# A new end for a hybrid decoder step: both normalisation factors as a power on GpSimd, low products last, all f32 products together, late scaling from two PSUM banks

## The chip, the core and the metric

The kernel runs on one core of one Trainium2 chip, as one program. The metric is the device time of one execution in microseconds (us). Three runs of the kernel before gave 1370.75, 1370.55 and 1371.1 us, so the median is 1370.75 us.

The engines are named as in the profile: PE (matrix products; PEld is its weight load), DVE (vector), ACT (scalar and activation functions), POOL (GpSimd), and SP, whose queue issues all of the transfers between main memory and the on-chip memory here. PSUM is the small memory in banks into which PE accumulates; an `acc` tile in this kernel is one bank of 128 partitions by 512 f32 numbers.

## The reference

One layer of a decoder step for 256 prompt tokens and 8 sample tokens, with 2048 features and everything in f32. The change concerns only the last lines, the residual of the channel mixer and the final normalisation:

```python
def rms_norm(x, g):
    xf = x.astype(jnp.float32)
    y = xf * lax.rsqrt(jnp.mean(xf * xf, axis=-1, keepdims=True) + EPS)
    return (y * g.astype(jnp.float32)).astype(x.dtype)
...
    x = x + (g_a * y_pool + g_b * y_lru + g_c * y_conf) @ w_out
    hid = jnp.square(jax.nn.relu(rms_norm(x, g_mlp) @ w_up))
    x = x + hid @ w_down
...
    y_prompt = rms_norm(xp, g_final)
    y_sample = rms_norm(xs, g_final)
```

So every token needs one number, its factor: the mean of its 2048 squares plus a small constant, to the power of minus one half. It can only be computed when the last of the 2048 features of that token is there.

## The kernel before, in words

**Layout.** All N = 264 tokens are worked on together. Activations lie feature by feature: the residual stream is `X`, 128 partitions by KD = 16 feature tiles by 264 tokens. Weights come in as a stream of chunks of 128 by 1024 numbers; ACT casts each into a high part `whi` and DVE subtracts to get the low part `wlo` (lines 223 and 224). An f32 product is made of three products of the rounded parts: high weight by high activation, low weight by high activation, high weight by low activation (`mm3`, line 250). An activation tile lies as a pair, 264 low numbers and then 264 high ones, and `rhs(k)` is this pair for k tile k. Four work queues are filled by hand in program order; on each engine instructions run in that order, and a semaphore wait holds up everything behind it on its engine.

**The last group.** The last four feature tiles of `w_down` (numbers 12, 13, 15, 14, in this order) are computed one after the other by `last_group`, so that each can be finished early; chunk c is half of a tile's 16 k tiles. For the last two (c = 4 to 7) the tokens are split. EARLY are the 136 tokens 128 to 263, LATE the 128 tokens 0 to 127. `early_mm` makes two products per k tile: the high weight with the EARLY columns of both activation parts (line 907; the two sums lie in columns 0 to 135 and 264 to 399 of the bank), and the low weight with all 264 high activations (line 908; columns 136 to 399). What is missing then for the LATE tokens are the two products with the high weight.

**The end** (`end`, called after chunk 7) finishes both kinds of tokens:
- EARLY tokens stay feature by feature. DVE adds the two sums of tile 14 to `X` (`plus`, line 911), squares them (line 1008); PE sums squares over partitions by a product with a matrix of 1/D (`early_sum`, line 951: once for `sq2`, which holds the squares of the other 15 tiles, once for tile 14). ACT takes the root of the mean (line 965, from a table of reciprocal roots loaded 1.28 us long at line 1189), DVE improves it by one Newton step (`early_factor`, lines 969 to 971), then multiplies `X` by it in five pieces, each followed by its store (`early_out`, lines 981 and 983).
- LATE tokens of the last two tiles are computed token by token: `late_rows` (line 961) uses the activations as weights and streams the high weights of both tiles, 32 products of 256 columns into the bank `turned`, whose first 256 columns are `pair`. `residual` (line 954) adds what is already in `X` by a product with the identity. Tiles 0 to 13 are turned by 14 transposes (`turn`, line 988) into four more banks. The squares of the first 14 tiles come from `sq2` by a product with one column (line 1002) and are copied by ACT (line 1003, `rest`); those of the pair by ACT with an accumulator (line 1021, `own`). ACT takes the root (line 965), DVE improves it in three steps on one column (`late_factor`, lines 975 to 977). ACT and DVE then scale the banks (lines 995, 993, 1030), and five stores follow (line 998).

The Newton step leaves out a factor of -1/2, which `gfin` (line 1146) and `last_gain` have in them instead.

Of the kernel before, what the change touches and what calls it, by code (L numbers as in the profile page):

```python
# [21 lines left out]
KD = D // P  # L22
EPS = 1e-6
LN_EXP = "natural_log_exp_and_others"
ROOT = "abs_reciprocal_sqrt_and_small"
GELU_C = 1.5957691216057308
GELU_K = 0.044715

# [65 lines left out]
def hybrid_step(ctx: ExitStack, tc: tile.TileContext, first, par_in, st_in, wall, y_out, st_out):  # L94
# [26 lines left out]
    gfin = cpool.tile([P, KD], F32, name="gfin")  # L121

    def pv(name, i=None, n=1):
        a, b = PCOL[name]
# [766 lines left out]
        later(1 + m % 4 // 2, one)  # L891
        later(2 + m % 4 // 2, other)

    ident = G[:, 12, :P]
    EARLY, NE = slice(P, N), N - P
    LATE = slice(0, P)
    wide = {}
# [3 lines left out]
    def apart(x):  # L901
        return x.rearrange("p (h n) -> p h n", h=2)

    def early_mm(ps, hi, lo, x, first, last):
        o = ps[:, :N + NE]
        both_sums = bass.AP(o.tensor, o.offset, [o.ap[0], [N, 2], [1, NE]])
        nc.tensor.matmul(both_sums, hi, apart(x)[:, :, EARLY], start=first, stop=False, skip_group_check=True)  # L907
        nc.tensor.matmul(ps[:, NE:NE + N], lo, x[:, N:], start=False, stop=last, skip_group_check=True)  # L908

    def plus(m, s, ps):  # L910
        nc.vector.tensor_tensor(X[:, m, s], X[:, m, s], ps, op=ALU.add)

    def gain(m, s):
        nc.scalar.activation(X[:, m, s], X[:, m, s], AF.Copy, scale=gfin[:, m:m + 1])

    def last_group(i, c, rhs, fn):
        t, k0 = c // 2, c % 2 * 8
        m = KD - 4 + LAST[t]
        if k0 == 0:
            wide[t] = acc()  # L920
        ps = wide[t]
        for k in range(k0, k0 + 8):
            s = slice((k - k0) * P, (k - k0 + 1) * P)
            hi, lo = whi[:, i % NHI, s], wlo[:, i % NHI, s]
            if c < 4:
                mm3(ps, hi, lo, rhs(k), k == 0, k == 15, MIXED)
            else:
                early_mm(ps, hi, lo, rhs(k), k == 0, k == 15)
        if c % 2 and t < 2:
            fn(t, ps)  # L930
        elif c == 5:
            plus(m, slice(0, N), ps[:, NE:NE + N])
            plus(m, EARLY, ps[:, :NE])
            nc.scalar.activation(squares[m][:, EARLY], X[:, m, EARLY], AF.Square)
            nc.gpsimd.tensor_tensor(sq2[:, EARLY], sq2[:, EARLY], squares[m][:, EARLY], op=ALU.add)
            gain(m, EARLY)
        elif c == 7:
            end(i, rhs)

    def end(i, rhs):  # L940
        assert i % NHI == 1 and NHI == 4
        m, fac, tn = KD - 2, G[:, 10, :], G[:, 9, :]
        unit = {}
        out = [cpool.tile([P, 4 * PITCH], F32, name=f"y{h}", tag=f"B{h}") for h in range(2)]
        turned, early, late = acc(), acc(), acc()
        pair = turned[:, :2 * P]
        halves = whi.rearrange("p (a b) c -> p a b c", a=2)
        own, rest, both_sq = late[:, 1:2], tn[:, 1:2], tn[:, 2:3]

        def early_sum(t, k):  # L950
            nc.tensor.matmul(early[:, :NE], ones, t[:, EARLY], start=k == 0, stop=k == 1)  # L951

        def residual(m, first, last):
            nc.tensor.matmul(turned[:, (m - KD + 2) * P:(m - KD + 3) * P], X[:, m, LATE], ident, start=first,  # L954
                             stop=last, skip_group_check=True)

        def late_rows(a, b):
            for k in range(a, b):
                w = halves[:, :, k // 8, k % 8 * P:k % 8 * P + P]
                for at in (0, N):  # L960
                    nc.tensor.matmul(apart(pair), rhs(k)[:, at:at + P], w, start=False, stop=False,  # L961
                                     skip_group_check=True)

        def root(dst, x, bias=0.0, scale=1.0):
            nc.scalar.activation(dst, x, AF.Abs_reciprocal_sqrt, bias=bias, scale=scale)

        def early_factor():
            s, r, t = early[:, :NE], rstd[:, EARLY], tn[:, EARLY]
            nc.vector.tensor_tensor(t, s, r, op=ALU.mult)
            nc.vector.tensor_tensor(t, t, r, op=ALU.mult)  # L970
            nc.vector.scalar_tensor_tensor(fac[:, EARLY], t, -3.0, r, op0=ALU.add, op1=ALU.mult)

        def late_factor():
            r = rstd[:, 0:1]
            nc.vector.scalar_tensor_tensor(both_sq, own, 1.0 / D, rest, op0=ALU.mult, op1=ALU.add)
            nc.vector.scalar_tensor_tensor(both_sq, both_sq, r, r, op0=ALU.mult, op1=ALU.mult)
            nc.vector.scalar_tensor_tensor(fac[:, 0:1], both_sq, -3.0, r, op0=ALU.add, op1=ALU.mult)

        def early_out(a, n):
            to = out[1][:, a * NE:(a + n) * NE]  # L980
            nc.vector.tensor_tensor(to.rearrange("p (k n) -> p k n", k=n), X[:, a:a + n, EARLY],
                                    fac[:, None, EARLY].to_broadcast([P, n, NE]), op=ALU.mult)
            nc.sync.dma_start(y_out[:, D + a * NE:D + (a + n) * NE], to)

        def turn(a, n):
            u = unit[a] = acc()
            for k in range(n):
                nc.tensor.transpose(u[:, k * P:(k + 1) * P], X[:, a + k, LATE], ident)  # L988

        def scale(eng, u, a, n):  # L990
            to, x, by = out[0][:, a * P:(a + n) * P], unit[u][:, (a - u) * P:(a - u + n) * P], fac[:, 0:1]
            if eng is nc.vector:
                nc.vector.tensor_scalar(to, x, by, None, op0=ALU.mult)  # L993
            else:
                nc.scalar.activation(to, x, AF.Copy, scale=by)  # L995

        def store(a, n):
            nc.sync.dma_start(y_out[:, a * P:(a + n) * P], out[0][:, a * P:(a + n) * P])

        ps = wide[3]  # L1000
        early_sum(sq2, 0)
        nc.tensor.matmul(late[:, :1], sq2[:, LATE], ones[:, :1], start=True, stop=True)  # L1002
# [5 lines left out]
        nc.vector.tensor_tensor(squares[m][:, EARLY], x, x, op=ALU.mult)  # L1008
# [12 lines left out]
        nc.scalar.activation(G[:, 14, :2 * P], pair, AF.Square, accum_out=own)  # L1021
# [8 lines left out]
        nc.vector.scalar_tensor_tensor(out[0][:, 14 * P:D], pair, fac[:, 0:1], last_gain, op0=ALU.mult, op1=ALU.mult)  # L1030
# [13 lines left out]
    def down_evac(q, m, whole):  # L1044
        into_x(m, whole)
        spend(dve=0.4)
        if q == 3:
            def rest():
                square_add(m)
                if m == 0:  # L1050
                    nc.gpsimd.tensor_scalar(sq2, sq2, 1.0, EPS * D / P, op0=ALU.mult, op1=ALU.add)  # L1051
                nc.scalar.activation(X[:, m, :], X[:, m, :], AF.Copy, scale=gfin[:, m:m + 1])

            later(0 if m >= KD - 4 else 1 + m % 4 // 2, rest)

# [79 lines left out]
    for i, ch in enumerate(chunks):  # L1135
# [6 lines left out]
        if i == 12:  # L1142
            softplus()
            again = first[:, KD:KD + 4 * HEAD].rearrange("p (k c) -> p k c", k=4)[:, :, :N]
            nc.sync.dma_start(X[:, 0:4, :], again)
            nc.vector.tensor_scalar(gfin, pv("g_final"), -0.5, None, op0=ALU.mult)
        if i % 2 == 0:
            dma_pair((i + 8) // 2)
        if i == 2:
# [32 lines left out]
            grp_mm(i)  # L1182
        if i == len(chunks) - 64:
            make_identity(nc, ident)
            nc.sync.dma_start(last_gain, par_in[:, NPAR:])
        if i == len(chunks) - 32:
            nc.scalar.activation(last_gain, last_gain, AF.Copy, scale=-0.5)
# [120 lines left out]
```

## Time and profile before

| what | us |
|---|---|
| median of three runs | 1370.75 |
| lowest and highest run | 1370.55, 1371.1 |
| span of the profiled execution, first to last instruction | 1368.7 |
| last product of the `early_mm` stream done | 1356.31 |
| last product on PE done (transposes) | 1362.75 |
| last instruction on DVE done | 1364.56 |
| transfers to main memory run dry | about 1367.2 |

The profile holds one execution, whose own time is given as its span, 1368.7 us; that is 2.05 us less than the median of the runs, which also count what lies before the first and after the last instruction. All times named with a decimal position such as "1356.31" are microseconds from the start of this span. A row of the timeline reads: start, duration, engine, line and operation, and in brackets how long the engine had been idle before and what ended it; consecutive instructions of one line are merged into one row. The chain of waits is a list of the work that ended last, with start and duration of each piece. A row of the table by stretches has the stretch, and for each engine its busy time and, in brackets, how many instructions; then the granted clock, the busy share of the transfer engines and what they moved in GB/s.

### The profile page before, as it was taken

The page shows a single profiled execution, that of the slowest core. Times are in us where ns is not written, and L with a number is a line of the kernel's source. Part 1 is how long each engine was busy: PE and PEld are TensorE (multiplying, and loading weights), DVE is VectorE, ACT ScalarE, POOL GpSimd, SP SyncE. Part 2 cuts the span into 40 slices and gives each one's busy share as a digit, 9 for nine tenths or more (in the row PEclk, how much of TensorE's full clock was granted, in tenths as well). Part 3 has the DMA queues.
Part 4 walks back from the last instruction along what each step waited for, and adds up shares of the span by engine and source line. Part 5 has one row for each costly group of instructions (what it writes and reads, how often), then busy time and mean ns, then how long its engine had stood idle before and what let it go on. Part 6 is the DMA issues. An engine that isn't in the chain of part 4 may idle for free.

```text
span 1368.7 us, 26945 instructions
## 1 busy us (share of the span) xinstructions
PE 1361.6 (99%) x11433; PEld 1360.2 (99%) x11433; DVE 894.8 (65%) x1470; ACT 729.4 (53%) x1069; POOL 86.1 (6%) x119
## 2 busy tenths in 40 slices
PE   9999999999999999999999999999999999999998
PEld 9999999999999999999999999999999999999998
DVE  7777888876877669666656455655465645465645
ACT  7757677657664646455544334543344533354544
POOL 0200010110102014011000000000000000000112
PEclk9999999999999999999999999999999999999999
DMA  8655555555565554555555555555555555555552
GB/s 322 226 180 186 185 191 192 186 181 187 186 212 188 185 185 169 200 183 186 187 186 185 185 185 185 185 185 184 186 185 185 185 185 185 190 185 185 185 186 95
DMA packets 41112, 257.64 MB, mean 188 GB/s; under 512 B 4512, under 2 KB 6944, under 8 KB 12064
## 3 DMA queue, kind: packets, MB, share of 16 engines
q1 hardware_dynamic: 40992, 255.93, 55.3%
q8 instruction: 89, 1.46, 0.4%
q14 instruction: 31, 0.25, 0.1%
HBM read 252.70 MB, written 3.21 MB: 187 GB/s over the span
## 4 chain that ended last, share of the span: by engine, by line
PE 99%; DMA 0%; ACT 0%; DVE 0%; DVEq 0%; issue 0%
PE acc L250 98%; PE acc L907 0%; PE acc L908 0%; PE acc L961 0%; DMA tmp<-first_dram 0%; PE acc L988 0%; DVE y L993 0%; PE acc L954 0%; PE acc L330 0%; ACT y L995 0%; PE acc L951 0%; ACT whi L233 0%; DVEq L1285 0%; PE acc L1002 0%
## 5 line engine op out<-in xcount | busy, mean ns | idle before, releaser
L224 DVE TENSOR_TENSOR wlo<-raw,whi 128x1024 fp32r<-128x1024 f32 (+1 forms) x478 | 580.7, 1217 | 434.4 <-ACT whi L223 433.6
L223 ACT CAST whi<-raw 128x1024 fp32r<-128x1024 f32 (+1 forms) x478 | 497.1, 1042 | 570.1 <-PE acc L250 502.2
L250 PE MATMUL acc<-A,whi 128*128 128x272 f32 (+2 forms) x3968 | 707.6, 281 | 0.4 <-ACT whi L233 0.4
L250 PEld LDWEIGHTS acc<-A,whi 128*128 128x128 f32 x3968 | 608.4, 188 | 0.6 <-ACT whi L233 0.6
L250 PE MATMUL acc<-A,wlo 128*128 128x264 f32 x1984 | 555.0, 282 | 0.0
L250 PEld LDWEIGHTS acc<-A,wlo 128*128 128x128 f32 x1984 | 370.8, 188 | 0.0
L250 PE MATMUL acc<-xn,whi 128*128 128x272 f32 (+1 forms) x2048 | 365.6, 281 | 0.0
L250 PEld LDWEIGHTS acc<-xn,whi 128*128 128x128 f32 x2048 | 314.4, 188 | 0.0
L250 PE MATMUL acc<-xn,wlo 128*128 128x264 f32 x1024 | 288.4, 282 | 0.0
L250 PEld LDWEIGHTS acc<-xn,wlo 128*128 128x128 f32 x1024 | 192.2, 188 | 0.0
L250 PE MATMUL acc<-Q,whi 128*128 128x272 f32 (+1 forms) x744 | 135.1, 281 | 0.0
L250 PE MATMUL acc<-LH,whi 128*128 128x272 f32 x736 | 133.1, 281 | 0.0
L250 PEld LDWEIGHTS acc<-Q,whi 128*128 128x128 f32 x744 | 115.2, 188 | 0.0
L250 PEld LDWEIGHTS acc<-LH,whi 128*128 128x128 f32 x736 | 113.7, 188 | 0.0
L250 PE MATMUL acc<-Q,wlo 128*128 128x264 f32 x372 | 104.8, 282 | 0.0
L250 PE MATMUL acc<-LH,wlo 128*128 128x264 f32 x368 | 103.6, 282 | 0.0
L250 PEld LDWEIGHTS acc<-Q,wlo 128*128 128x128 f32 x372 | 69.8, 188 | 0.0
L250 PEld LDWEIGHTS acc<-LH,wlo 128*128 128x128 f32 x368 | 69.1, 188 | 0.0
L647 ACT ACTIVATE G<-tmp,par 128x256 f32<-128x256 f32 x120 | 54.4, 501 | 8.0 <-DVE G L650 7.1
L1051 POOL TENSOR_SCALAR G<-G 128x264 f32<-128x264 f32 x1 | 0.4, 417 | 656.8 <-ACT G L867 656.8
L650 DVE TENSOR_TENSOR G<-G 128x1024 f32<-128x1024 f32 x30 | 38.2, 1275 | 0.0
L167 DVE TENSOR_TENSOR acc<-acc,side 128x8 f32<-128x8 f32 x188 | 32.5, 173 | 6.9 <-ACT side L164 1.9
(216 smaller groups left out, 653.7 us busy)
## 6 DMA issues: line engine op xcount, KB each, us to landing
raw<-wall_dram SPq DMA_DIRECT2D x226, 1024.0 KB, 4.9
raw<-wall_dram SPq DMA_DIRECT2D x12, 512.0 KB, 6.2
raw<-first_dram SPq DMA_DIRECT2D x6, 512.0 KB, 8.1
X<-first_dram SPq DMA_DIRECT2D x6, 264.0 KB, 7.7
raw<-wall_dram SPq DMA_DIRECT2D x5, 256.0 KB, 3.4
tmp<-first_dram SPq DMA_DIRECT2D x3, 388.0 KB, 4.6
y_dram<-y SPq DMA_DIRECT2D x3, 272.0 KB, 2.3
y_dram<-y SPq DMA_DIRECT2D x3, 256.0 KB, 2.3
```

The source lines that it names most:

```text
L167: nc.vector.tensor_tensor(ps[:, N:N + TS], ps[:, N:N + TS], t, op=ALU.add)
L223: nc.scalar.copy(h[:, s], r[:, s])
L224: nc.vector.tensor_tensor(lo[:, s], r[:, s], f(h[:, s]), op=ALU.subtract)
L250: nc.tensor.matmul(ps[:, o:o + b - a], lo if low_w else hi, x[:, a:b], start=start, stop=stop, skip_group_check=True)
L647: nc.scalar.activation(dst[:, ct, :TP], vext[:, ct, k:k + TP], AF.Copy, scale=par[:, w:w + 1])
L650: nc.vector.tensor_tensor(VC[:, :, :TP], VC[:, :, :TP], src[:, :, :TP], op=ALU.add)
L1051: nc.gpsimd.tensor_scalar(sq2, sq2, 1.0, EPS * D / P, op0=ALU.mult, op1=ALU.add)
```

## The change

Six things change, all around the end:
- Both factors are a power of -1/2, computed by a tensor operation on POOL. EARLY: ACT copies the mean out of PSUM (`early_mean`), POOL raises 128x136 numbers (`early_factor`). LATE: POOL adds `rest` and `own` and raises one column (`late_factor`). The roots on ACT, their table load, the Newton steps on DVE and the factor -1/2 in the gains go.
- `last_early` makes the second chunk of the last tile in another order: k tiles 0 to 3 of it as before, then the four high products of k tiles 4 to 7, then their four low products. DVE adds the sum that only high products touch first.
- The five f32 products (two `early_sum`, two `residual`, the one-column product) stand in one row on PE, after the first six products of `late_rows`, which now open the bank.
- `rest` is copied later by ACT.
- EARLY output is cut into four pieces instead of five.
- LATE scaling: ACT starts on the bank of tiles 0 to 3, DVE on that of tiles 4 to 7; there are three stores instead of five, of 2, 6 and 8 tiles.

```diff
@@ the last group
-    def early_mm(ps, hi, lo, x, first, last):
+    def early_high(ps, hi, x, first):
         o = ps[:, :N + NE]
         both_sums = bass.AP(o.tensor, o.offset, [o.ap[0], [N, 2], [1, NE]])
         nc.tensor.matmul(both_sums, hi, apart(x)[:, :, EARLY], start=first, stop=False, skip_group_check=True)
+
+    def early_low(ps, lo, x, last):
         nc.tensor.matmul(ps[:, NE:NE + N], lo, x[:, N:], start=False, stop=last, skip_group_check=True)
+
+    def early_mm(ps, hi, lo, x, first, last):
+        early_high(ps, hi, x, first)
+        early_low(ps, lo, x, last)
+
+    def last_early(i, ps, rhs):
+        hi, lo = whi[:, i % NHI, :], wlo[:, i % NHI, :]
+        for k in range(4):
+            s = slice(k * P, (k + 1) * P)
+            early_mm(ps, hi[:, s], lo[:, s], rhs(8 + k), False, False)
+        for k in range(4, 8):
+            early_high(ps, hi[:, k * P:(k + 1) * P], rhs(8 + k), False)
+        for k in range(4, 8):
+            early_low(ps, lo[:, k * P:(k + 1) * P], rhs(8 + k), k == 7)
...
@@ in end()
-        def root(dst, x, bias=0.0, scale=1.0):
-            nc.scalar.activation(dst, x, AF.Abs_reciprocal_sqrt, bias=bias, scale=scale)
+        def early_mean():
+            nc.scalar.copy(tn[:, EARLY], early[:, :NE])
 
         def early_factor():
-            s, r, t = early[:, :NE], rstd[:, EARLY], tn[:, EARLY]
-            nc.vector.tensor_tensor(t, s, r, op=ALU.mult)
-            nc.vector.tensor_tensor(t, t, r, op=ALU.mult)
-            nc.vector.scalar_tensor_tensor(fac[:, EARLY], t, -3.0, r, op0=ALU.add, op1=ALU.mult)
+            nc.gpsimd.tensor_tensor(fac[:, EARLY], tn[:, EARLY], power.to_broadcast([P, NE]), op=ALU.pow)
 
         def late_factor():
-            r = rstd[:, 0:1]
-            nc.vector.scalar_tensor_tensor(both_sq, own, 1.0 / D, rest, op0=ALU.mult, op1=ALU.add)
-            nc.vector.scalar_tensor_tensor(both_sq, both_sq, r, r, op0=ALU.mult, op1=ALU.mult)
-            nc.vector.scalar_tensor_tensor(fac[:, 0:1], both_sq, -3.0, r, op0=ALU.add, op1=ALU.mult)
+            nc.gpsimd.tensor_tensor(own, own, rest, op=ALU.add)
+            nc.gpsimd.tensor_tensor(fac[:, 0:1], own, power, op=ALU.pow)
...
         ps = wide[3]
-        early_sum(sq2, 0)
-        nc.tensor.matmul(late[:, :1], sq2[:, LATE], ones[:, :1], start=True, stop=True)
-        nc.scalar.copy(rest, late[:, :1])
-        residual(m + 1, True, False)
+        plus(m, EARLY, ps[:, :NE])
         plus(m, EARLY, ps[:, N:N + NE])
-        plus(m, EARLY, ps[:, :NE])
         x = X[:, m, EARLY]
         nc.vector.tensor_tensor(squares[m][:, EARLY], x, x, op=ALU.mult)
+        plus(m, LATE, ps[:, NE:NE + P])
         gain(m, EARLY)
-        plus(m, LATE, ps[:, NE:NE + P])
         late_rows(0, 3)
+        nc.tensor.matmul(late[:, :1], sq2[:, LATE], ones[:, :1], start=True, stop=True)
+        residual(m + 1)
+        early_sum(sq2, 0)
         early_sum(squares[m], 1)
-        root(rstd[:, EARLY], early[:, :NE])
+        residual(m)
+        nc.scalar.copy(rest, late[:, :1])
+        early_mean()
+        early_factor()
         late_rows(3, 16)
-        residual(m, False, True)
-        early_factor()
-        for a, n in ((0, 2), (2, 4), (6, 4), (10, 4), (14, 2)):
+        for a, n in ((0, 2), (2, 4), (6, 5), (11, 5)):
             early_out(a, n)
         for a, n in ((0, 4), (4, 4), (8, 4), (12, 2)):
             turn(a, n)
-        nc.scalar.activation(G[:, 14, :2 * P], pair, AF.Square, accum_out=own)
-        root(rstd[:, 0:1], own, rest, 1.0 / D)
+        nc.scalar.activation(G[:, 14, :2 * P], pair, AF.Square, scale=D ** -0.5, accum_out=own)
         late_factor()
         scale(nc.scalar, 0, 0, 2)
-        scale(nc.vector, 0, 2, 2)
+        scale(nc.vector, 4, 4, 4)
         store(0, 2)
-        store(2, 2)
-        scale(nc.scalar, 4, 4, 4)
-        store(4, 4)
+        scale(nc.scalar, 0, 2, 2)
+        store(2, 6)
         nc.vector.scalar_tensor_tensor(out[0][:, 14 * P:D], pair, fac[:, 0:1], last_gain, op0=ALU.mult, op1=ALU.mult)
+        scale(nc.scalar, 8, 8, 4)
         scale(nc.vector, 12, 12, 2)
-        store(12, 4)
-        scale(nc.scalar, 8, 8, 4)
-        store(8, 4)
+        store(8, 8)
...
@@ in the loop over chunks
-        if i == len(chunks) - 4:
-            nc.scalar.preload_act_table_set(ROOT)
```

What the change moves shows best in the order in which instructions stand on an engine; line numbers of the changed kernel differ a little from those before. On PE, before, from the last product of the `early_mm` stream on (names: `G,ones` is `early_sum`, `ones,G` the one-column product, `G,X` a `residual` or a transpose, `whi,LH` and `whi,Q` are `late_rows`):

```order
L908 MATMUL acc<-Q,wlo 128x264
L951 MATMUL acc<-G,ones 128x136 [waits PE_49,Pool_49]
L1002 MATMUL acc<-ones,G 128x1 [waits PE_49]
L954 MATMUL acc<-G,X 128x128 [waits DMAHW6_49,DVE_49]
L961 MATMUL acc<-whi,LH 128x256 x6
L951 MATMUL acc<-G,ones 128x136 [waits DVE_49]
L961 MATMUL acc<-whi,LH 128x256 x10
L961 MATMUL acc<-whi,Q 128x256 x16
L954 MATMUL acc<-G,X 128x128 [waits DVE_49]
```

and now:

```order
L905 MATMUL acc<-Q,whi 128x2x136 x4
L908 MATMUL acc<-Q,wlo 128x264 x4
L977 MATMUL acc<-whi,LH 128x256 [waits PE_49]
L977 MATMUL acc<-whi,LH 128x256 x5
L1019 MATMUL acc<-ones,G 128x1 [waits PE_49,Pool_49]
L970 MATMUL acc<-G,X 128x128 [waits DMAHW6_49,DVE_49]
L967 MATMUL acc<-G,ones 128x136 [waits PE_49,Pool_49]
L967 MATMUL acc<-G,ones 128x136 [waits DVE_49]
L970 MATMUL acc<-G,X 128x128 [waits DVE_49]
L977 MATMUL acc<-whi,LH 128x256 x10
L977 MATMUL acc<-whi,Q 128x256 x16
```

The same products stand there; three f32 products went behind the first six rows of `late_rows`, and the last `residual` came forward from behind all 32 of them. `early_sum` of tile 14 has the same work ahead of it as before.

On DVE, from the squares of tile 14 to the end, before (`y` are the two output buffers, one for EARLY and one for LATE):

```order
L1008 TENSOR_TENSOR G<-X 128x136 [waits DVE_49]
L911 TENSOR_TENSOR X<-X,acc 128x128
L969 TENSOR_TENSOR G<-acc,rstd 128x136 [waits Activation_49]
L970 TENSOR_TENSOR G<-G,rstd 128x136 [waits DVE_49]
L971 SCALAR_TENSOR_TENSOR G<-G,rstd 128x136 [waits DVE_49]
L981 TENSOR_TENSOR y_14658<-X,G 128x272 [waits DVE_49]
L981 TENSOR_TENSOR y_14658<-X,G 128x544 x3
L981 TENSOR_TENSOR y_14658<-X,G 128x272
L975 SCALAR_TENSOR_TENSOR G<-acc,G 128x1 [waits Activation_49]
L976 SCALAR_TENSOR_TENSOR G<-G,rstd 128x1 [waits DVE_49]
L977 SCALAR_TENSOR_TENSOR G<-G,rstd 128x1 [waits DVE_49]
```

and now DVE down to its first scaling, and behind it POOL's last four instructions (the sum for `sq2`, the two powers and the addition between them):

```order
L1015 TENSOR_TENSOR G<-X 128x136 [waits DVE_49]
L925 TENSOR_TENSOR X<-X,acc 128x128
L992 TENSOR_TENSOR y_14655<-X,G 128x272 [waits Pool_49]
L992 TENSOR_TENSOR y_14655<-X,G 128x544
L992 TENSOR_TENSOR y_14655<-X,G 128x680
L992 TENSOR_TENSOR y_14655<-X,G 128x680 [waits Activation_49]
L1004 TENSOR_SCALAR y_14654<-acc,G 128x512 [waits PE_49,Pool_49]
```

```order
L951 TENSOR_TENSOR G<-G 128x136 [waits Activation_49,Pool_49]
L984 TENSOR_TENSOR G<-G 128x136 [waits DVE_49,Activation_49]
L987 TENSOR_TENSOR G<-G 128x1 [waits DVE_49,Activation_49]
L988 TENSOR_TENSOR G<-G 128x1 [waits Pool_49]
```

Six DVE instructions went, and DVE now waits for POOL at two places: ahead of the first EARLY output and ahead of its first LATE scaling.

On SP the stores at the end, before:

```order
L983 DMA y_dram<-y_14658 128x272 [waits DVE_49]
L983 DMA y_dram<-y_14658 128x544 [waits DVE_49] x3
L983 DMA y_dram<-y_14658 128x272 [waits DVE_49]
L998 DMA y_dram<-y_14657 128x256 [waits DMAHW5_49,Activation_49]
L998 DMA y_dram<-y_14657 128x256 [waits DMAHW6_49,DVE_49]
L998 DMA y_dram<-y_14657 128x512 [waits DMAHW7_49,Activation_49]
L998 DMA y_dram<-y_14657 128x512 [waits DMAHW0_49,DVE_49]
L998 DMA y_dram<-y_14657 128x512 [waits DMAHW1_49,Activation_49]
```

and now:

```order
L994 DMA y_dram<-y_14655 128x272 [waits DVE_49]
L994 DMA y_dram<-y_14655 128x544 [waits DVE_49]
L994 DMA y_dram<-y_14655 128x680 [waits DVE_49] x2
L1009 DMA y_dram<-y_14654 128x256 [waits Activation_49]
L1009 DMA y_dram<-y_14654 128x768 [waits DMAHW5_49,DVE_49,Activation_49]
L1009 DMA y_dram<-y_14654 128x1024 [waits DMAHW6_49,DVE_49,Activation_49]
```

Ten stores became seven of the same bytes, and the LATE stores still stand behind all the EARLY ones.

More of the change, by code (lines that the diff above doesn't have):

```diff
@@ L892, in up_evac @@
         later(2 + m % 4 // 2, other)
-    ident = G[:, 12, :P]
+    ident, power = G[:, 12, :P], G[:, 12, P:P + 1]
     EARLY, NE = slice(P, N), N - P
@@ L913, in gain @@
     def gain(m, s):
[L914 removed]
+        nc.scalar.activation(X[:, m, s], X[:, m, s], AF.Copy, scale=pv("g_final", m))
     def last_group(i, c, rhs, fn):
@@ L947, in end, with residual @@
         halves = whi.rearrange("p (a b) c -> p a b c", a=2)
-        own, rest, both_sq = late[:, 1:2], tn[:, 1:2], tn[:, 2:3]
+        own, rest = tn[:, 0:1], tn[:, 1:2]
         def early_sum(t, k):
             nc.tensor.matmul(early[:, :NE], ones, t[:, EARLY], start=k == 0, stop=k == 1)
-        def residual(m, first, last):
-            nc.tensor.matmul(turned[:, (m - KD + 2) * P:(m - KD + 3) * P], X[:, m, LATE], ident, start=first,
-                             stop=last, skip_group_check=True)
+        def residual(m):
+            nc.tensor.matmul(turned[:, (m - KD + 2) * P:(m - KD + 3) * P], X[:, m, LATE], ident, start=False,
+                             stop=False, skip_group_check=True)
         def late_rows(a, b):
```

14 lines of the change are left out of this document (6 added, 8 removed).

## The prediction

> **What bounds the kernel now.** I read the page's shares first, then the busy times by stretch, then the chain of waits of the end.
>
> ```profile
> span 1368.7 us, 26945 instructions
> PE 1361.6 (99%) x11433; PEld 1360.2 (99%) x11433; DVE 894.8 (65%) x1470; ACT 729.4 (53%) x1069; POOL 86.1 (6%) x119
> ```
>
> ```profile
> 0.00:1356.31 1356.31, 1355.18 (x11379) 1353.97 (x11380) 888.30 (x1452) 726.20 (x1060) 86.06 (x119) 1.00 0.56 188
> ...
> 1362.75:1364.56 1.81, 0.00 (x0) 0.00 (x0) 1.27 (x3) 1.63 (x3) 0.00 (x0) 1.00 0.80 294
> ```
>
> PE is busy for 1355.18 of the first 1356.31 us, and in that stretch the change removes only work of other engines (a table load, two small scalings); it keeps the number of products. So nothing is to be won there, and everything is decided in the last 12.4 us (1368.7 - 1356.31). A difference that a measurement of this kernel can tell is about 0.2%, 2.74 us, more than a fifth of that end. The chain shows the end's PE part:
>
> ```profile
> 1356.31 0.23 PE acc L951 x2
> 1356.54 0.12 PE acc L1002 x2
> 1356.66 0.33 PE acc L954 x2
> 1356.99 0.71 PE acc L961 x6
> 1357.70 0.23 PE acc L951 x2
> 1357.93 3.05 PE acc L961 x26
> 1360.98 0.22 PE acc L954 x2
> 1361.20 1.54 PE acc L988 x14
> ```
>
> PE stops at 1362.75, yet the span goes on for 6 us. The stretches cut by what the transfers do say why (the last two numbers of a row are their busy share and GB/s):
>
> ```profile
> 1359.76:1360.60 0.84, 0.84 (x10) 0.84 (x9) 0.84 (x2) 0.00 (x0) 0.00 (x0) 1.00 0.00 0
> ...
> 1361.60:1363.20 1.60, 1.13 (x11) 0.89 (x9) 0.93 (x5) 0.83 (x5) 0.00 (x0) 1.00 1.02 385
> ...
> 1363.70:1365.20 1.50, 0.00 (x0) 0.00 (x0) 0.86 (x3) 0.71 (x2) 0.00 (x0) 1.00 0.66 225
> 1365.20:1367.20 2.00, 0.00 (x0) 0.00 (x0) 0.00 (x0) 0.00 (x0) 0.00 (x0) 0.67 1.01 382
> 1367.20:1368.70 1.50, 0.00 (x0) 0.00 (x0) 0.00 (x0) 0.00 (x0) 0.00 (x0) 0.50 0.02 5
> ```
>
> Two waves of output, 1.1 MB EARLY and 1.05 MB LATE, each run the transfers full (385 and 382 GB/s) when there is enough to move; between them they run at 225 GB/s because the LATE pieces come slowly. They run dry at 1367.2, and 1.5 us of closing follow, which stay. So I ask of each edit when it lets the two waves start, and whether they can still run at 383 GB/s.
>
> **The change part by part.** The rows of the end on DVE, ACT and SP:
>
> ```profile
> 1356.35 0.63 DVE L911 TENSOR_TENSOR X<-X,acc 128x136 f32<-128x136 f32 x2 [3.16 <-PE acc L908]
> 1357.01 0.30 DVE L1008 TENSOR_TENSOR G<-X 128x136 f32<-128x136 f32 x1
> ...
> 1357.97 0.28 ACT L965 ACTIVATE rstd<-acc 128x136 f32<-128x136 f32 x1 [0.22 <-PE acc L951]
> 1358.29 0.30 DVE L969 TENSOR_TENSOR G<-acc,rstd 128x136 f32<-128x136 f32 x1 [0.78 <-ACT rstd L965]
> ...
> 1359.29 2.70 DVE L981 TENSOR_TENSOR y<-X,G 128x272 f32<-128x272 f32 x5
> ...
> 1361.30 0.39 ACT L1021 ACTIVATE G<-acc 128x256 f32<-128x256 f32 x1 [3.05 <-PE acc L954]
> 1361.58 0.17 ACT L1021 ACTIVATION_READ_ACCUMULATOR G<-acc 128x1 f32 x1
> ...
> 1362.78 1.63 ACT L995 ACTIVATE y<-acc,G 128x256 f32<-128x256 f32 x3 [0.74 <-PE acc L988]
> 1363.29 0.48 DVE L993 TENSOR_SCALAR y<-acc,G 128x256 f32<-128x256 f32 x1 [0.60 <-ACT y L995]
> 1363.69 0.48 DVE L1030 SCALAR_TENSOR_TENSOR y<-acc,G 128x256 f32<-128x256 f32 x1
> ```
>
> ```profile
> 1359.76 0.98 SPq L983 DMA_DIRECT2D y_dram<-y  x2
> ...
> 1363.28 2.34 SPq L998 DMA_DIRECT2D y_dram<-y  x5
> ```
>
> *High products first: 0.* It could let DVE add its first sum 0.5 us sooner, beside the four low products. But PE wants the squares of tile 14 only at 1357.70, behind the first six rows of `late_rows`, and DVE had them at 1357.31 (1357.01 + 0.30): 0.39 us of slack on either side of the edit. Besides, in the built program the count that DVE's first addition waits for is raised by the last low product, not by the last high one, so I expect it at 1356.35 as before.
>
> *f32 products in a row: 0.* L951, L1002, L954 take ten passes in 0.23 + 0.12 + 0.33 + 0.23 + 0.22 = 1.13 us, 0.113 us each; L961 takes 3.05/26 = 0.117 us. A change between the two kinds shows no price (at most the 0.11 us by which the first L954 is longer than the second). The sum in front of `early_sum` of tile 14 stays 0.23 + 0.12 + 0.33 + 0.71 us, and the pair is complete after the same 4.89 us, at 1361.20. The last `residual` needs DVE's LATE addition, done by 1357.51, and stands at about 1357.93: no wait.
>
> *EARLY factor.* Before: mean at 1357.93, root, three DVE steps, first output at 1359.29. Now ACT copies 128x136 (0.28 us, from L965's row), ending at 1358.25, then POOL. What POOL's rows give:
>
> ```profile
> 1353.28 0.32 ACT L934 ACTIVATE G<-X 128x136 f32<-128x136 f32 x1 [0.83 <-DVE X L911]
> ...
> 1353.74 0.47 POOL L935 TENSOR_TENSOR G<-G 128x136 f32<-128x136 f32 x1 [3.18 <-ACT G L934]
> ```
>
> ```profile
> L750 POOL COPY st<-qtmp 128x60 f32<-128x60 f32 x1 | 1.2, 1236 | 17.2 <-DVE qtmp L725 17.2
> L502 POOL COPY st<-tmp 128x24 f32<-128x24 f32 x1 | 1.2, 1203 | 3.8 <-DVE tmp L466 3.8
> ...
> L579 POOL COPY st<-tmp 128x64 f32<-128x64 f32 x1 | 0.5, 513 | 0.1
> L935 POOL TENSOR_TENSOR G<-G 128x136 f32<-128x136 f32 x1 | 0.5, 474 | 3.2 <-ACT G L934 3.2
> L1051 POOL TENSOR_SCALAR G<-G 128x264 f32<-128x264 f32 x1 | 0.4, 417 | 656.8 <-ACT G L867 656.8
> L415 POOL TENSOR_TENSOR G<-G 128x8 f32<-128x8 f32 x1 | 0.2, 206 | 42.2 <-DVE gfin L1146 42.2
> ...
> L424 POOL TENSOR_SCALAR sp<-G 128x8 f32<-128x8 f32 x1 | 0.2, 197 | 0.1
> ```
>
> The step from ACT to POOL is 0.14 us (1353.28 + 0.32 to 1353.74), so POOL starts at 1358.39. The power itself, c, no row shows. Below, it costs no less than an addition of this shape, 0.47 us. Above, I count steps: L1051 multiplies and adds 264 columns in 417 ns, L424 does it for 8 in 197, so a pair of such steps costs 220/256 = 0.86 ns per column. A power is a logarithm and an exponential; the kernel's own logarithm (lines 418 to 421) takes ten turns. Twenty pairs give 0.2 + 136 x 17.2 ns = 2.5 us, forty give 4.9 us. The dearest row per column, L750, has 20.6 ns, which would be 2.8 us. I take 24 pairs, ten for each series and four to part and join exponents: **c = 3.0 us**, all of it on the path. A step of 0.1 us to DVE is an estimate (0.04 us from ACT to DVE at L969). DVE starts its outputs at 1358.49 + c and, at the same 2.70 us for the same columns, ends at E = 1361.19 + c = 1364.19, against 1361.99 before.
>
> *What waits behind it.* DVE's queue holds the four outputs and then all of its LATE scaling; SP's queue holds the LATE stores behind the EARLY ones. From the third EARLY store on, the transfers are then full: it is issued at about E - 0.84 (the last 680 of 2176 columns) and moves 0.84 us later (1359.76 to 1360.60), at E. What is left is two stores of 680 columns and 256 + 768 + 1024 LATE columns, 3408 x 512 bytes = 1.745 MB, at 383 GB/s 4.56 us. The last store does not come too late for that: DVE scales 512 columns in 0.8 us (two steps of 0.40, from 1363.29 to 1363.69), then 256 and 256, until E + 1.73; its data can move at E + 2.6, and its turn is at E + 3.2. So the transfers run dry at E + 4.56 = 1365.75 + c, which is 1368.75, against 1367.20: **+1.55 us**, or c - 1.45 in general.
>
> *LATE factor.* The squares are summed at 1361.75 (1361.58 + 0.17); POOL starts at 1361.89, adds in 0.2 us (L415), raises one column in 0.2 us or more, so ACT scales from about 1362.4 instead of 1362.78. With c = 3.0 that lies under the EARLY wave and is worth nothing.
>
> *Two banks and three stores.* Before, DVE's first scaling waited 0.60 us for ACT on the same bank; now it need not. This counts only if DVE is free, with a small c: then the stores can issue at about 1362.9, 1363.3 and 1364.15, and their 128, 384 and 512 KiB run dry at 1366.6, **0.6 us sooner** than before. That is the most that the whole change can gain.
>
> Sum for the likeliest case: 0 + 0 + 1.55 = 1.55 us on the span, 1368.7 to 1370.25. Runs lie 2.05 us above the profiled span (1370.75 - 1368.7), so 1370.75 + 1.55 = **1372.3 us**: slower, but inside 0.2%.
>
> **The rivals.**
> - *A cheap power*, c under 1.45 us: the EARLY wave starts as early as before and the LATE edits pay. For it: POOL is idle and a one-pass addition costs 0.47 us. Against it: a power is no single step in software. Time 1370.2 to 1370.75.
> - *A long power*, c over 4.2 us: slower by over 2.74 us. The same place, POOL at 1358.39, with 40 pairs or with columns that do not overlap in time; forty pairs give 4.9 - 1.45 = 3.4 us and 1374.2 us, double that price 9.6 - 1.45 = 8.1 us and 1378.9 us. For it: in L1051 the next column does not need the one before, while a series is one chain of steps, each of which needs the last. Against it: nothing but the count. [...] No row of this trace shows such a chain.
> - *A dear first use.* The first COPY took 1203 ns for 24 columns, a later one 513 ns for 64: 0.7 us more. A power that pays this has c = 3.7 and gives 1373.0 us. Against it: POOL's first TENSOR_TENSOR (L415, 206 ns) shows nothing of the sort. [...]
>
> **How the numbers follow.** The forecast, c between 1.45 and 4.2, has 0.48 and its own range 1370.75 to 1373.5; the cheap power 0.20; the long one 0.27; the dear first use 0.05, half of it over the bound. Faster by over 0.2% would need 2.74 us where at most 0.6 can be had: 0.01. Within 0.2%: 0.48 + 0.20 + 0.02 = 0.70. Slower: 0.27 + 0.02 = 0.29. The range goes from the gain of 0.6 us to c = 6.7, 1370.1 to 1376.0; what is beyond are the dearest powers, about 0.1.
>
> **What would show it.** In the changed kernel's profile: the new TENSOR_TENSOR of 128x136 on POOL, 3 us long from 1358.4; DVE waiting for it some 3.2 us after the LATE addition; the EARLY outputs ending near 1364.2; transfers at 380 GB/s without a gap until 1368.7; PE's end at 1362.75 as before; DVE's first addition still at the last low product. I am wrong if DVE ends its EARLY outputs at 1362 (the cheap power) or after 1365.4 (the long one), if PE waits inside the end, or if the transfers fall under 350 GB/s with the fewer, larger stores.

## The result: 20.55 us slower, all of it in one instruction on POOL

| kernel | median us | runs |
|---|---|---|
| before | 1370.79 | 1370.55 to 1371.1, 5 runs |
| changed | 1391.34 | 1391.17 to 1391.64, 5 runs |

The ratio is 1.015, with a 95% interval of 1.0138 to 1.0161: 20.55 us slower where 1.55 us had been forecast. The profiled span went from 1368.7 to 1389.1 us.

The page's shares of the changed kernel hold PE as busy as before, and 23 us more on POOL (109.0 against 86.1):

```profile
span 1389.1 us, 26935 instructions
PE 1361.7 (98%) x11433; PEld 1360.2 (98%) x11433; DVE 893.3 (64%) x1462; ACT 726.9 (52%) x1066; POOL 109.0 (8%) x123
```

The timeline of its end, by engine, first POOL, then DVE, then ACT:

```profile
1358.34 22.08 POOL L984 TENSOR_TENSOR G<-G 128x136 f32<-128x136 f32 x1 [4.11 <-ACT G L981]
1380.40 0.19 POOL L987 TENSOR_TENSOR G<-G 128x1 f32<-128x1 f32 x1
1380.67 0.65 POOL L988 TENSOR_TENSOR G<-G 128x1 f32<-128x1 f32 x1
```

```profile
1356.38 0.63 DVE L925 TENSOR_TENSOR X<-X,acc 128x136 f32<-128x136 f32 x2 [3.17 <-PE acc L908]
...
1380.46 2.63 DVE L992 TENSOR_TENSOR y<-X,G 128x272 f32<-128x272 f32 x4 [22.92 <-POOL G L984]
1383.01 0.75 DVE L1004 TENSOR_SCALAR y<-acc,G 128x512 f32<-128x512 f32 x1
```

```profile
1361.54 0.19 ACT L1032 ACTIVATION_READ_ACCUMULATOR G<-acc 128x1 f32 x1
1381.35 1.42 ACT L1006 ACTIVATE y<-acc,G 128x256 f32<-128x256 f32 x3 [19.62 <-POOL G L988]
```

L984 is the EARLY power. It takes 22.08 us, and both other engines wait for it: DVE 22.92 us with all of its outputs behind that wait, and ACT, whose sum of LATE squares was ready at 1361.73, 19.62 us, because the LATE addition and power (L987, L988) stand behind L984 in POOL's queue. The stretches of the changed kernel show the transfers after that:

```profile
1356.34:1380.46 24.12, 6.41 (x57) 6.17 (x55) 1.09 (x5) 1.20 (x5) 22.12 (x2) 0.69 0.00 0
1380.46:1383.09 2.63, 0.00 (x0) 0.00 (x0) 2.63 (x5) 1.42 (x3) 0.78 (x2) 0.50 0.41 149
1383.09:1384.54 1.45, 0.00 (x0) 0.00 (x0) 1.45 (x4) 0.00 (x0) 0.00 (x0) 0.50 1.00 390
1384.54:1387.60 3.06, 0.00 (x0) 0.00 (x0) 0.00 (x0) 0.00 (x0) 0.00 (x0) 0.50 1.01 392
1387.60:1389.10 1.50, 0.00 (x0) 0.00 (x0) 0.00 (x0) 0.00 (x0) 0.00 (x0) 0.50 0.02 6
```

Nothing moves until 1380.46; from the end of DVE's EARLY outputs at 1383.09 the transfers run full without a gap for 4.5 us, and 1.5 us of closing follow, as before.

One measure is used below to compare ends free of the start of the span: the time from DVE's first addition for the last tile (line 911 before, L925 in the changed kernel) to the end of the span. It is 1368.7 - 1356.35 = 12.35 us before and 1389.1 - 1356.38 = 32.72 us in the changed kernel, 20.37 us more. It is read from one profiled execution of each kernel, whose span is given to 0.1 us.

### The profile page after: what moved, and what is told of

Read it like the earlier page. It is cut to its first block, busy times and chain, and to the rows that moved or that the text cites. A ratio compares the mean times of both kernels' runs of the same rounds, so it can differ in the third digit from the quotient of the medians.

```text
span 1389.1 us, 26935 instructions
## 1 busy us (share of the span) xinstructions
PE 1361.7 (98%) x11433; PEld 1360.2 (98%) x11433; DVE 893.3 (64%) x1462; ACT 726.9 (52%) x1066; POOL 109.0 (8%) x123
## 4 chain that ended last, share of the span: by engine, by line
PE 97%; POOL 2%; DVE 0%; issue 0%; DMA 0%; ACT 0%; DVEq 0%; POOLq 0%; ACTq 0%
PE acc L248 97%; POOL G L984 2%; DMA tmp<-first_dram 0%; DVE y L992 0%; DVE wlo L222 0%; DVE y L1004 0%; ACT whi L221 0%; DVEq L1289 0%; DVE X L925 0%; ACT X L1060 0%; PE acc L328 0%; POOL G L951 0%; DVE X L1049 0%; ACT G L865 0%; ACT whi L231 0%
## 5 line engine op out<-in xcount | busy, mean ns | idle before, releaser
L867 POOL TENSOR_TENSOR G<-G 128x264 f32<-128x264 f32 x28 | 27.3, 975 | 122.1 <-ACT G L865 121.2
```

What stands on the lines that cost most here:

```text
L867: nc.gpsimd.tensor_tensor(sq2, sq2, t, op=ALU.add)
```

## The experiments

Two theories stood for the 22 us: a price per column, and a dear first use of the power. Two runs were made to tell them apart; then come runs on what sets the price per column, and on what the other edits are worth without it. "Before" was run again beside every group.

### A power used early

```diff
             nc.gpsimd.memset(power, -0.5)
+            nc.gpsimd.tensor_tensor(G[:, 12, P + 1:P + 2], ones[:, 0:1], power, op=ALU.pow)
```

> The changed kernel with one more power, of a single column of ones, on POOL some 64 chunks before the end, so that the code of a power has been used long before the EARLY factor needs it. Theory 1, a price per column: (22.08 - 0.65) / 135 = 0.159 us per column, so the 128x136 power stays at 22.1 us, the early single one takes 0.65 us, and the time stays at 1391.3 us. Theory 2, a dear first use of some 21 us: the early single power takes it, the 128x136 power falls to 1 or 2 us, and the time falls to about 1371.

Measured: 1391.47 us, one run. The groups of POOL's instructions of this run:

```profile
L984 POOL TENSOR_TENSOR G<-G 128x136 f32<-128x136 f32 x1 | 22.1, 22072 | 4.1 <-ACT G L981 4.1
...
L988 POOL TENSOR_TENSOR G<-G 128x1 f32<-128x1 f32 x1 | 0.6, 634 | 0.1
...
L1193 POOL TENSOR_TENSOR G<-ones,G 128x1 f32<-128x1 f32 x1 | 0.6, 581 | 0.1
```

The first power of the program, L1193, takes 0.58 us, and the wide one stays at 22.07 us. There is no dear first use.

### Two halves

```diff
-            nc.gpsimd.tensor_tensor(fac[:, EARLY], tn[:, EARLY], power.to_broadcast([P, NE]), op=ALU.pow)
+            for s in (slice(P, P + NE // 2), slice(P + NE // 2, N)):
+                nc.gpsimd.tensor_tensor(fac[:, s], tn[:, s], power.to_broadcast([P, NE // 2]), op=ALU.pow)
```

> The changed kernel with the EARLY power made as two powers of 68 columns each. Theory 1, a price per column: 0.49 + 68 x 0.159 = 11.3 us for each of the two, 22.6 us together, and the time within 1 us of 1391.3. Theory 2, a dear first use: the first takes over 20 us, the second under 1.5 us.

Measured: 1391.98 us, one run, and in the groups of POOL:

```profile
L985 POOL TENSOR_TENSOR G<-G 128x68 f32<-128x68 f32 x2 | 22.4, 11230 | 4.1 <-ACT G L981 4.1
```

Half the columns take 11.23 us in the mean of the two; how the 22.4 us divide between them this row does not say, so against a dear first use stands the run above. With one column at 0.65 us and 136 at 22.08, three widths lie nearly on one line: (22.08 - 0.65) / 135 = 0.159 us per column, and 0.65 + 67 x 0.159 = 11.3 us for 68.

### A multiplication in the power's place

```diff
-            nc.gpsimd.tensor_tensor(fac[:, EARLY], tn[:, EARLY], power.to_broadcast([P, NE]), op=ALU.pow)
+            nc.gpsimd.tensor_tensor(fac[:, EARLY], tn[:, EARLY], power.to_broadcast([P, NE]), op=ALU.mult)
```

> The changed kernel with a multiplication on POOL in the place of the 128x136 power (so the EARLY tokens' power of -1/2 is left out and they are scaled by another number); the detour over ACT's copy and POOL, and all other edits, stay. Theory 1 and 2 alike, that the power alone made it slower: POOL takes 0.47 us there, DVE's outputs start at about 1359.0 instead of 1380.5, the transfers run dry at about 1367.0, and the time is 1370.2 to 1370.8 us. Rival, that the detour or the new order costs by itself: over 1372 us.

Measured: 1370.56 us over 10 runs, against 1370.63 for before in the same group; ratio 0.9998, interval 0.9989 to 1.0007. The timeline of POOL and DVE:

```profile
1358.49 0.41 POOL L984 TENSOR_TENSOR G<-G 128x136 f32<-128x136 f32 x1 [4.11 <-ACT G L981]
```

```profile
1356.53 0.62 DVE L925 TENSOR_TENSOR X<-X,acc 128x136 f32<-128x136 f32 x2 [3.17 <-PE acc L908]
...
1358.94 2.63 DVE L992 TENSOR_TENSOR y<-X,G 128x272 f32<-128x272 f32 x4 [1.26 <-POOL G L984]
```

With 0.41 us in the place of 22.08 the loss is gone, and the end is 1368.3 - 1356.53 = 11.77 us long, 0.58 us shorter than before (the median, which also holds everything ahead of the end, is lower by only 0.07 us). The way over ACT's copy and POOL costs nothing that the time shows; the power itself, with 22.08 us, costs all of the 20 us.

### 16 partitions

```diff
-            nc.gpsimd.tensor_tensor(fac[:, EARLY], tn[:, EARLY], power.to_broadcast([P, NE]), op=ALU.pow)
+            nc.vector.tensor_copy(fac[:, EARLY], tn[:, EARLY])
+            nc.gpsimd.tensor_tensor(fac[:16, EARLY], tn[:16, EARLY], power[:16].to_broadcast([16, NE]), op=ALU.pow)
```

> The changed kernel with the EARLY power over 16 partitions of 136 columns only; the other 112 partitions get a plain copy of the mean, so there the EARLY tokens' power is left out. [...] Rival, a price per number, partitions one after the other: 22.08 x 16 / 128 = 2.8 us.

Measured: 1391.2 us, one run, and POOL's group:

```profile
L985 POOL TENSOR_TENSOR G<-G 16x136 f32<-16x136 f32 x1 | 22.1, 22069 | 4.4 <-DVE G L984 4.4
```

An eighth of the numbers takes the same time, 22.07 us against 22.08 on 128 partitions, and not the 2.8 us of a price per number. So of these two counts the price does not hang on the number of partitions; others were not tried. The EARLY factor is laid out badly for that: 136 columns, the same in all 128 partitions, while the LATE factor is one column of 128 different numbers, raised in 0.65 us.

### A written exponent, and an exponent of one

```diff
# the first
-            nc.gpsimd.tensor_tensor(fac[:, EARLY], tn[:, EARLY], power.to_broadcast([P, NE]), op=ALU.pow)
+            nc.gpsimd.tensor_tensor(fac[:, EARLY], tn[:, EARLY], G[:, 15, :NE], op=ALU.pow)
...
+            nc.gpsimd.memset(G[:, 15, :NE], -0.5)
# the second
+    one_power = G[:, 12, P + 1:P + 2]
...
-            nc.gpsimd.tensor_tensor(fac[:, EARLY], tn[:, EARLY], power.to_broadcast([P, NE]), op=ALU.pow)
+            nc.gpsimd.tensor_tensor(fac[:, EARLY], tn[:, EARLY], one_power.to_broadcast([P, NE]), op=ALU.pow)
...
+            nc.gpsimd.memset(one_power, 1.0)
```

> The changed kernel with the exponent of the EARLY power read from a written tile of 136 columns instead of one column repeated. Theory, the power itself is dear: 22.1 us as before, time 1391.3. Rival, the repeated operand is what makes it dear: under 5 us and a time under 1375.

> The changed kernel with the EARLY exponent 1 instead of -1/2 (so the EARLY tokens are scaled by their mean square and their factor is left out). Theory, every column goes through the whole logarithm and exponential whatever the exponent: 22.1 us again. Rival, that the price hangs on the numbers, and an exponent of 1 is passed through: under 5 us, and a time under 1375.

Measured: 1390.96 and 1390.9 us, one run each. The power in the first and in the second:

```profile
L984 POOL TENSOR_TENSOR G<-G 128x136 f32<-128x136 f32 x1 | 22.1, 22140 | 4.1 <-ACT G L981 4.1
```

```profile
L985 POOL TENSOR_TENSOR G<-G 128x136 f32<-128x136 f32 x1 | 22.1, 22080 | 4.1 <-ACT G L982 4.1
```

Neither the repeated operand nor an exponent of 1 instead of -1/2 changes the price.

### The EARLY factor as before, the rest as changed

```diff
+ROOT = "abs_reciprocal_sqrt_and_small"
...
-            nc.scalar.copy(tn[:, EARLY], early[:, :NE])
+            nc.scalar.activation(rstd[:, EARLY], early[:, :NE], AF.Abs_reciprocal_sqrt)
...
-            nc.gpsimd.tensor_tensor(fac[:, EARLY], tn[:, EARLY], power.to_broadcast([P, NE]), op=ALU.pow)
+            s, r, t = early[:, :NE], rstd[:, EARLY], tn[:, EARLY]
+            nc.vector.scalar_tensor_tensor(t, s, -0.5, r, op0=ALU.mult, op1=ALU.mult)
+            nc.vector.tensor_tensor(t, t, r, op=ALU.mult)
+            nc.vector.scalar_tensor_tensor(fac[:, EARLY], t, 1.5, r, op0=ALU.add, op1=ALU.mult)
...
+        if i == len(chunks) - 4:
+            nc.scalar.preload_act_table_set(ROOT)
```

> The changed kernel with the EARLY factor made as in the kernel before, by ACT's root and one Newton step on DVE (written so that no factor of -1/2 is left over); the LATE factor stays a power of one column on POOL and all other edits stay. If the 128x136 power is the whole loss: outputs from 1359.3 on as before; LATE factor at 1361.87 + 0.27 + 0.65 = 1362.8, as before; from DVE's free start on a second bank and three stores some 0.2 us sooner than before, 1370.4 to 1370.8 us. If another edit costs too: over 1371.2.

Measured: 1370.13 us over 11 runs against 1370.63; ratio 0.9996, interval 0.9987 to 1.0005. That is below the 1370.4 to 1370.8 us expected: banks and stores had been counted with 0.2 us. Its timeline, DVE and POOL:

```profile
1356.58 0.62 DVE L926 TENSOR_TENSOR X<-X,acc 128x136 f32<-128x136 f32 x2 [3.17 <-PE acc L909]
```

```profile
1362.01 0.19 POOL L991 TENSOR_TENSOR G<-G 128x1 f32<-128x1 f32 x1 [7.57 <-ACT G L1036]
1362.28 0.56 POOL L992 TENSOR_TENSOR G<-G 128x1 f32<-128x1 f32 x1
```

The end is 1368.4 - 1356.58 = 11.82 us, 0.53 us shorter than before. The runs scatter by 1.2 us, so the interval holds no difference too; the shorter end is read from the trace.

### No power at all

To the edit above comes, for the LATE factor:

```diff
-            nc.gpsimd.tensor_tensor(own, own, rest, op=ALU.add)
-            nc.gpsimd.tensor_tensor(fac[:, 0:1], own, power, op=ALU.pow)
+            r, h = rstd[:, 0:1], tn[:, 2:3]
+            nc.scalar.activation(r, own, AF.Abs_reciprocal_sqrt, bias=rest)
+            nc.vector.tensor_scalar(h, own, rest, -0.5, op0=ALU.add, op1=ALU.mult)
+            nc.vector.scalar_tensor_tensor(h, h, r, r, op0=ALU.mult, op1=ALU.mult)
+            nc.vector.scalar_tensor_tensor(fac[:, 0:1], h, 1.5, r, op0=ALU.add, op1=ALU.mult)
```

> The changed kernel without any power: both factors by ACT's root and one Newton step on DVE; the order of the products, the row of f32 products, the two banks and the stores stay as changed. If a power of one column on POOL (0.27 + 0.56 us) costs what root and three steps on DVE cost (1.03 us from the sum of squares to the first scaling in the kernel before, 0.95 in the run with the LATE power): within 0.2 us of that run, 1369.9 to 1370.4 us. If the LATE power itself was the gain of that run: back at 1370.6.

Measured: 1370.24 us over 11 runs against 1370.76; ratio 0.9996, interval 0.9988 to 1.0005.

```profile
1356.87 0.62 DVE L926 TENSOR_TENSOR X<-X,acc 128x136 f32<-128x136 f32 x2 [3.17 <-PE acc L909]
```

The end is 1368.7 - 1356.87 = 11.83 us, that of the run above. So a power of one column on POOL costs what it replaces, as far as these traces tell, and the 0.5 us come from elsewhere.

### Only the two banks and three stores

```diff
         scale(nc.scalar, 0, 0, 2)
-        scale(nc.vector, 0, 2, 2)
+        scale(nc.vector, 4, 4, 4)
         store(0, 2)
-        store(2, 2)
-        scale(nc.scalar, 4, 4, 4)
-        store(4, 4)
+        scale(nc.scalar, 0, 2, 2)
+        store(2, 6)
...
-        scale(nc.vector, 12, 12, 2)
-        store(12, 4)
         scale(nc.scalar, 8, 8, 4)
-        store(8, 4)
+        scale(nc.vector, 12, 12, 2)
+        store(8, 8)
```

> The kernel before with nothing changed but the LATE scaling: DVE starts on the bank of tiles 4 to 7 while ACT works on that of tiles 0 to 3, and three stores of 2, 6 and 8 tiles instead of five. In the runs with all the small edits the span from the last low product to the end was 0.5 us shorter than before (11.86 against 12.39 us). Theory: all of that is this edit; so 11.9 us here, DVE no longer waiting 0.60 us for ACT, and some 0.5 us less than before in the same runs. Rival, that the order of the products or the later copy give part of it: 12.1 us or more here.

Measured: 1370.24 us over 11 runs against 1370.89; ratio 0.9996, interval 0.9987 to 1.0005. The timeline of DVE, ACT and SP:

```profile
1356.58 0.62 DVE L911 TENSOR_TENSOR X<-X,acc 128x136 f32<-128x136 f32 x2 [3.16 <-PE acc L908]
...
1363.02 0.75 DVE L993 TENSOR_SCALAR y<-acc,G 128x512 f32<-128x512 f32 x1
```

```profile
1363.01 1.42 ACT L995 ACTIVATE y<-acc,G 128x256 f32<-128x256 f32 x3 [0.73 <-PE acc L988]
```

```profile
1363.51 1.44 SPq L998 DMA_DIRECT2D y_dram<-y  x3
```

DVE starts with ACT instead of 0.51 us after it, its wait for ACT is gone from the waits, and the three stores are issued in 1.44 us where the five took 2.34. The end is 1368.5 - 1356.58 = 11.92 us: 0.43 of the 0.53 us. That leaves 0.1 us for the order of the products, the later copy of `rest` and the four EARLY pieces together, which is no more than the last decimal of a span. The two banks and the three stores were not tried apart.

### Logarithm and exponential on ACT, with all other edits

```diff
-            nc.scalar.copy(tn[:, EARLY], early[:, :NE])
+            nc.scalar.activation(tn[:, EARLY], early[:, :NE], AF.Ln)
...
-            nc.gpsimd.tensor_tensor(fac[:, EARLY], tn[:, EARLY], power.to_broadcast([P, NE]), op=ALU.pow)
+            nc.scalar.activation(fac[:, EARLY], tn[:, EARLY], AF.Exp, scale=-0.5)
...
-            nc.gpsimd.tensor_tensor(own, own, rest, op=ALU.add)
-            nc.gpsimd.tensor_tensor(fac[:, 0:1], own, power, op=ALU.pow)
+            nc.scalar.activation(own, own, AF.Ln, bias=rest)
+            nc.scalar.activation(fac[:, 0:1], own, AF.Exp, scale=-0.5)
```

> The changed kernel with both powers on ACT instead of POOL, as a logarithm and an exponential of -1/2 of it, from the table that is loaded already; so the Newton step of the kernel before is left out as well, and the factor is as exact as these two functions are. Two ACT instructions of some 0.28 us on 136 columns put the first EARLY output at about 0.65 us after the mean where root and Newton took 1.36; two of 0.26 us on one column let the LATE scaling start 0.6 us after its sum instead of 1.03. Expected, if the LATE path sets the end: 0.4 us less than the run with the LATE power, 1369.5 to 1370.0. If the EARLY wave of transfers set the end, the gain would be about 0.7 us.

Measured: 1369.9 us over 11 runs against 1370.76; ratio 0.9993, interval 0.9984 to 1.0002. The timeline of DVE and ACT:

```profile
1356.66 0.63 DVE L925 TENSOR_TENSOR X<-X,acc 128x136 f32<-128x136 f32 x2 [3.17 <-PE acc L908]
```

```profile
1358.28 0.28 ACT L981 ACTIVATE G<-acc 128x136 f32<-128x136 f32 x1 [0.17 <-PE acc L967]
1358.60 0.32 ACT L984 ACTIVATE G<-G 128x136 f32<-128x136 f32 x1
...
1362.05 0.29 ACT L987 ACTIVATE G<-G 128x1 f32<-128x1 f32 x1
1362.37 0.20 ACT L988 ACTIVATE G<-G 128x1 f32<-128x1 f32 x1
```

The same power of 128x136 numbers takes 0.28 + 0.32 us here, 22.08 us on POOL. The end is 1368.1 - 1356.66 = 11.44 us, 0.91 us shorter than before and the shortest of all. Against the run with the EARLY root it is 0.38 us shorter, the 0.4 us expected if the LATE path sets the end, and not the 0.7 us of the other case. This kernel is 21.4 us faster than the changed one; against the kernel before its median is 0.86 us lower, and the interval just holds no difference.

### Logarithm and exponential alone

The same two factors in the kernel before, with its own order of products, scaling and five stores:

```diff
-            nc.scalar.activation(dst, x, AF.Abs_reciprocal_sqrt, bias=bias, scale=scale)
+            nc.scalar.activation(dst, x, AF.Ln, bias=bias, scale=scale)
...
+            nc.scalar.activation(fac[:, EARLY], rstd[:, EARLY], AF.Exp, scale=-0.5)
...
+            nc.scalar.activation(fac[:, 0:1], rstd[:, 0:1], AF.Exp, scale=-0.5)
```

(the Newton steps on DVE, the root table and the factors of -1/2 go).

> The kernel before with nothing changed but the two factors: logarithm and exponential on ACT from the table that is loaded already, no root table, no Newton step; products, scaling and the five stores as before. With all other edits this took another 0.4 us off the end (11.48 against 11.86 us). Theory, that the gains are on one path and add: from the sum of the LATE squares to the first LATE scaling 0.6 instead of 1.03 us, and an end of 12.0 us here against 12.39. Rival, that with five stores the transfers and not the factor set the end: 12.3 us or more.

Measured: 1370.21 us over 11 runs against 1370.89; ratio 0.9995, interval 0.9987 to 1.0004.

```profile
1356.63 0.62 DVE L911 TENSOR_TENSOR X<-X,acc 128x136 f32<-128x136 f32 x2 [3.17 <-PE acc L908]
```

The end is 1368.4 - 1356.63 = 11.77 us, 0.58 us shorter than before, and rather more than the 0.39 us expected (12.0 us). With the 0.43 us of banks and stores it makes 1.01 us, of which 0.91 were there together: the gains lie on one path and nearly add. The rival, that five stores hide it, falls.

**Where the gains lie.** ACT's first LATE scaling cuts each end in two. Its rows with the multiplication, the EARLY root, both roots, logarithm and exponential with all other edits, and the same alone:

```profile
1362.83 1.42 ACT L1006 ACTIVATE y<-acc,G 128x256 f32<-128x256 f32 x3 [0.95 <-POOL G L988]
```

```profile
1362.88 1.42 ACT L1010 ACTIVATE y<-acc,G 128x256 f32<-128x256 f32 x3 [0.95 <-POOL G L992]
```

```profile
1363.19 1.42 ACT L1013 ACTIVATE y<-acc,G 128x256 f32<-128x256 f32 x3 [0.64 <-DVE G L995]
```

```profile
1362.61 1.42 ACT L1006 ACTIVATE y<-acc,G 128x256 f32<-128x256 f32 x3
```

```profile
1362.54 1.63 ACT L989 ACTIVATE y<-acc,G 128x256 f32<-128x256 f32 x3
```

From DVE's first addition to that scaling it is 6.43 us before and with banks and stores alone, 6.30, 6.30 and 6.32 us in the first three of these runs, 5.95 and 5.91 us in the last two. From there to the end of the span it is 5.92 and 5.86 us in the two kernels with five stores, and 5.47 to 5.52 us in the five with three, although with the multiplication the EARLY outputs start 0.53 us sooner than with the EARLY root. So the LATE path sets the end in all seven; banks and stores shorten what follows the scaling, the factor what lies before it, and so does the 0.1 us left over. The medians, 0.07 to 0.86 us below before, do not confirm so fine a split: by them banks and stores alone gain 0.65 us, and with the other edits and the EARLY root 0.50.

## Why the prediction was wrong

**The price of the power: wrong by seven times.** The step that failed is the term c = 3.0 us of "EARLY factor". It measured 22.08 us. The way to it was the row of a multiply and an add on POOL, 0.86 ns per column for a pair; at 24 pairs, 159 ns per column is 6.6 ns a pair. The prediction itself named the doubt, that in that row no column needs the one before while a series is a chain, but priced it only up to twice forty pairs, 9.6 us, and left everything over 6.7 us outside the range as about one chance in ten. The bound from above was the weak place. L750, a copy with 20.6 ns per column, was taken for the dearest row per column, but L502, which the prediction shows beside it, has 1203 / 24 = 50 ns, which would be 6.8 us; even that is less than a third of what came. Nothing says that an instruction of a kind that the trace lacks should lie near any that it has. That a power on POOL is two series, and of how many steps, was the author's estimate, and whether a chain of steps is what fills the 159 ns no run here shows. Shown is that the columns set the price (0.65, 11.23 and 22.08 us for 1, 68 and 136 of them), and that it stays between 22.07 and 22.14 us on 16 partitions, with an exponent of 1, with a written operand and after an earlier use.

**The dear first use: not there.** The first power of the run with an early one took 0.58 us, a later one of the same width there 0.63. The copies that the rival was read from do not bear it out either: L750 is the second of them and took 1236 ns for 60 columns, as long as the first with 1203 ns for 24. Half of its chance of 0.05 was put over the 0.2% bound, but the 0.7 us of the copies gave 1373.0 us, which is inside it; no run shows a first use that would cost more.

**The sum around it: right.** The general form was c - 1.45 us. With the measured c it gives 22.08 - 1.45 = 20.6 us; the runs show 20.55 and the spans 20.4. The outputs were to end at E = 1361.19 + c = 1383.27 and ended at 1383.09; the transfers were to run dry 4.56 us after, and did so 4.5 us after, at 390 to 392 GB/s where 383 had been taken. So the rival of a long power, with a chance of 0.27, had the right place, the right queue behind it and the right price per microsecond of c; only its size was cut off at 9.6 us.

**High products first: right, 0.** DVE's first addition came at 1356.38 in the changed kernel, released by the low products of L908, as before.

**f32 products in a row: right, 0.** The run with the EARLY root gives the chain of waits on PE, from the last low products on:

```profile
1356.55 0.71 PE acc L978 x6
1357.25 0.12 PE acc L1023 x2
1357.37 0.33 PE acc L971 x2
1357.70 0.46 PE acc L968 x4
1358.16 0.22 PE acc L971 x2
1358.38 3.05 PE acc L978 x26
```

The ten passes in a row take 0.12 + 0.33 + 0.46 + 0.22 = 1.13 us, exactly what they took apart, and no product waits.

**LATE factor: right in kind, a little off in size.** The one-column power took 0.56 to 0.66 us instead of 0.2 or more. So the LATE scaling starts as late with it as with root and Newton step (6.30 and 6.32 us after DVE's first addition), not about 0.4 us sooner.

**Two banks and three stores: right.** 0.6 us was named as the most; 0.43 us was measured alone and 0.53 to 0.58 with the other edits.

## What to carry to other kernels

An operation that the trace has never shown on an engine is to be measured by itself before it goes on the path that sets the end; here the neighbouring rows bounded it from below only. For the power on POOL the layout decided: 128 numbers in one column took 0.65 us, 136 numbers in 136 columns, repeated over all partitions, 22.08 us, and ACT made them 37 times faster by two functions of 0.28 and 0.32 us. And an end that is a queue of waits can be summed in terms of its one unknown; here that sum held, to 0.2 us, at seven times the size that had been put into it.

## What the runs showed of the hardware that was not expected

- The power on POOL cost 0.159 us per column between 1 and 136 columns, the same on 16 and on 128 partitions (22.07 and 22.08 us), for the exponents 1 and -1/2 (22.08 us both) and for a written operand (22.14 us); one column took 0.56 to 0.66 us. A multiplication of the same 128x136 took 0.41 us, so the power was 54 times dearer.
- ACT's logarithm and exponential took 0.28 and 0.32 us for the same shape.
- From the first issue to the end of the last, waits for data included, five stores took 2.34 us and three of the same bytes 1.44 us; in the changed kernel the larger ones still moved at 390 GB/s.
